# RWKV-7 scan on one TensorE: one 128x192 product for a chunk's masked products and transposes

## The chip, the cores and the metric

The kernel runs on one core of one Trainium2 chip. The time is the device time of one execution in microseconds (us), as the median of three runs. A profile of one further execution shows what each engine did: TensorE (PE, with its weight loads as PEld), VectorE (DVE), ScalarE (ACT), GpSimd (POOL), and SyncE (SP), whose queue issues most DMAs.

## The reference, cut to what matters

The program is a two-layer encoder for 256 + 1024 tokens of width 1024 in float32: an RWKV-7 layer, a neighbourhood attention layer, each followed by an MLP with 4096 hidden channels. The change concerns the recurrence of the first layer. For each of 16 heads and both directions of time it computes

```python
def step(S, inp):
    r_t, w_t, k_t, v_t, a_t, b_t = inp
    sa = jnp.einsum('bhvk,bhk->bhv', S, a_t)
    S = S * w_t[:, :, None, :] + sa[..., None] * b_t[:, :, None, :] + v_t[..., None] * k_t[:, :, None, :]
    return S, jnp.einsum('bhvk,bhk->bhv', S, r_t)
```

with a 64x64 state S per head. The output y of both directions is added, normalised per head (group norm with gain `lnx_g` and offset `lnx_b`), and a bonus times v is added to it.

## The kernel before

**Stages.** `l0_proj` makes r, k, v and the decay factors of all tokens and stores four scaled copies a, r (in `ar_d`) and b, k (in `bk_d`) to DRAM, per channel tile of 128 (two heads), direction and token. `scan` runs the recurrence. `channel_layer` and `attention` do the rest, and the change leaves them alone.

**The scan.** Time is cut into chunks of L = 64 tokens. Within a chunk the recurrence is products of 64x64 matrices; only the state S goes from chunk to chunk. Two heads lie in partitions 0 to 63 and 64 to 127, so a step's products are 64x64 quarters of the TensorE array; `HALVES` lists the two halves `es` and the opposite ones `eo`. There are ten jobs (`scan_job`) of 16 chunks, each job in 16 steps (`scan_step`); one step treats one chunk forward and one backward. The chunks of a job come in groups of four, g = 0 to 3, per direction d.

**What each (d, g) needs before its steps.** `prod` (L806) makes the masked a-b products; POOL and DVE then invert them (`mtr`, `rank1`, `qst`, some 36 steps ahead), and `merge1` and `merge2` (L899, L910) complete the inverse Q. `kload` (L928) loads r and k; a and b are still in SBUF from `load` (L801). `kprod` (L934) makes the products b-r into the bank `bps` and k-a, k-r into the bank `kps`; DVE multiplies them with the causal masks into `zr` (L951) and `zk` (L948). `ktr` (L953) transposes b and k through products with the identity into `lbps` and `lkps`; ACT copies them out as `lb` and `lk` (L964).

**One step** (L1005 to L1068): `s0` multiplies masked products and transposed k with v, ahead of time; `s1` multiplies a and r with the state S and adds S itself through the identity into the next state's bank `sn`; `s1c` copies the sum on ACT (`up`, L1034); `s2` multiplies Q with `up`; `s2c` copies it on ACT (`u`, L1045); `s3` multiplies transposed b and masked b-r with `u`; `s3c` scales `sn` into the new S on ACT (L1060, one instruction per direction); `s4` stores or adds the output y (L1066, L1068). S, `up`, `u`, S is a serial loop between PE and ACT.

**After eight chunks** `scan_post` normalises y on DVE and ACT, turns y and the bonus with `tr` (L1132, 16 products of 64x64 each) into `zps` and `vps`, applies gain and offset on ACT (`trc`, L1141), adds on DVE (`p5`, L1145) and stores with two DMAs (L1147).

**What sets the order.** In this stage every piece is put on a list with a time in steps, `at(t, f)`; the list is sorted by time and written out under `manual_schedule`, so each of PE, DVE, ACT and POOL runs its instructions in that written order. SP issues its DMAs in the order of the list too. Every engine stops at an instruction whose input or buffer isn't ready, and what is behind it waits.

**PSUM.** Eight banks: three in rotation under the tag `aps` (pool `pa`, for `aps`, `yps`, `qps`, `bps`, `kps`, `lbps`, `lkps`, `zps`, `vps`), one for A, two each for Y and for `sn` with U.

Of the kernel before, what the change touches and what calls it, by code (L numbers as in the profile page):

```python
# [29 lines left out]
V_QG, V_KG, V_LG, V_LB = 136, 137, 138, 146  # L30
NVEC = 154
# [18 lines left out]
class Trunk:  # L50
# [50 lines left out]
    def l0_proj(self):  # L101
# [253 lines left out]
        self.pa = self.pt = self.sctx.enter_context(tc.tile_pool(name="pa", bufs=3, space=PSUM, reuse_waits="tile"))  # L355
# [50 lines left out]
        def rmm(m, s):  # L406
            c0, c1 = SEGS[s]
            ps = ev[m, s] = self.pa.tile([P, 512], F32, name="rps", tag="aps")
# [37 lines left out]
        def vmm(i):  # L446
            q, tb = i // 10, i % 10
            vw = [tuple(z[:, k % 2 * 256:k % 2 * 256 + 256] for z in wq["v", q, k // 2]) for k in range(KT)]
            ev[i] = self.v_block(act, vw, v_d, (vp, "vt", 256, 2), (self.pa, "aps"), q, tb, later=True)
# [49 lines left out]
    def v_block(self, act, vw, dst, tp, pp, q, tb, scale=1.0, later=False):  # L499

        nc = self.nc
        ps = pp[0].tile([P, 512], F32, name="vps", tag=pp[1])
# [210 lines left out]
    def scan_begin(self):  # L713
# [10 lines left out]
        self.r_aa, self.r_bb, self.r_za = ([[er.tile([P, 4, 64], F32, name=f"{name}{i}") for i in range(9)], 0] for name in ("aa", "bb", "za"))  # L724
# [19 lines left out]
    def scan(self):  # L744
# [10 lines left out]
        for r, name in ((self.r_aa, "aa"), (self.r_bb, "bb"), (self.r_za, "za")):  # L755
            grow(r, name, [P, 4, 64], 12)
# [5 lines left out]
        self.b_a = self.pw.tile([P, 512], F32, name="ba")  # L762
        self.b_y, self.b_s = ([self.pw.tile([P, 512], F32, name=f"{nm}{i}") for i in range(2)] for nm in ("by", "bs"))
# [13 lines left out]
    def scan_job(self, j):  # L777
# [19 lines left out]
        for n, (d, g) in enumerate(order):  # L797
# [3 lines left out]
            def load(d=d, g=g, m=m, c0=c0):  # L801
                J["aa", d, g], J["bb", d, g] = self.nxt(self.r_aa), self.nxt(self.r_bb)
                nc.sync.dma_start(J["aa", d, g], c4(self.ar_d[m, d, 0, :, tok(c0)]))
                nc.sync.dma_start(J["bb", d, g], c4(self.bk_d[m, d, 0, :, tok(c0)]))

            def prod(h, d=d, g=g):  # L806
                if h == 0:
                    J["pa"] = w4(self.pa.tile([P, 512], F32, name="aps", tag="aps"))
                if h < 2:
                    for c in (2 * h, 2 * h + 1):  # L810
                        for es, eo in HALVES:
                            mm(J["pa"][es, c], J["bb", d, g][es, c], J["aa", d, g][es, c], start=True, stop=True)  # L812
# [83 lines left out]
        for n, (d, g) in enumerate(order):  # L896
# [27 lines left out]
            for dt, f in ((0.7, lambda f=merge1: f(0)), (0.72, lambda f=merge1: f(2)), (1.2, merge1c), (1.7, lambda f=merge2: f(0)), (1.72, lambda f=merge2: f(2)), (2.2, merge2c)):  # L924
                at(t + dt, f)


            def kload(d=d, g=g, m=m, c0=c0):  # L928
                J["rr", d, g] = self.rp.tile([P, 4, 64], F32, name="rr", tag="rr", bufs=8)
                nc.sync.dma_start(J["rr", d, g], c4(self.ar_d[m, d, 1, :, tok(c0)]))  # L930
                J["kk", d, g] = self.rp.tile([P, 4, 64], F32, name="kk", tag="kk", bufs=3)
                nc.sync.dma_start(J["kk", d, g], c4(self.bk_d[m, d, 1, :, tok(c0)]))

            def kprod(h, d=d, g=g):  # L934
                aa, rr, bb, kk = (J[x, d, g] for x in ("aa", "rr", "bb", "kk"))
                if h == 0:
                    J["pb"] = w4(self.pa.tile([P, 512], F32, name="bps", tag="aps"))
                    J["pk"] = self.pa.tile([P, 4, P], F32, name="kps", tag="aps")
                if h < 2:
                    for c in (2 * h, 2 * h + 1):  # L940
                        for es, eo in HALVES:
                            mm(J["pb"][es, c], bb[es, c], rr[es, c], start=True, stop=True)
                            mm(J["pk"][eo, c, 0:64], kk[es, c], aa[es, c], start=True, stop=True)
                        for es, eo in HALVES:
                            mm(J["pk"][eo, c, 64:128], kk[es, c], rr[es, c], start=True, stop=True)
                elif h == 2:
                    zk = J["zk", d, g] = self.rp.tile([P, 4, P], F32, name="zk", tag="zk", bufs=5)
                    nc.vector.tensor_tensor(out=zk, in0=J["pk"], in1=b4(self.mask[d], P), op=ALU.mult)  # L948
                else:
                    zr = J["zr", d, g] = self.rp.tile([P, 4, 64], F32, name="zr", tag="zr", bufs=5)  # L950
                    nc.vector.tensor_tensor(out=zr, in0=J["pb"], in1=b4(self.mask[d][:, 64:128], 64), op=ALU.mult)  # L951

            def ktr(h, d=d, g=g):  # L953
                if h == 0:
                    J["pl"] = [w4(self.pa.tile([P, 512], F32, name=nm, tag="aps")) for nm in ("lbps", "lkps")]
                if h < 2:
                    for c in (2 * h, 2 * h + 1):
                        for es, eo in HALVES:
                            mm(J["pl"][0][es, c], J["bb", d, g][es, c], self.ident[es, es], start=True, stop=True)
                            mm(J["pl"][1][eo, c], J["kk", d, g][es, c], self.ident[es, es], start=True, stop=True)  # L960
                else:
                    nm = ("lb", "lk")[h - 2]
                    lt = J[nm, d, g] = self.rp.tile([P, 4, 64], F32, name=nm, tag=nm, bufs=5)
                    nc.scalar.copy(lt, J["pl"][h - 2])  # L964
            t = 2 * n - 6
            at(t - 3.0, kload)
            for h, (dt, dl) in enumerate(((0.06, 1.4), (0.65, 1.41), (0.8, 1.65), (0.81, 1.85))):
                at(t + dt, lambda h=h, f=kprod: f(h))
                at(t + dl, lambda h=h, f=ktr: f(h))
# [21 lines left out]
    def scan_step(self, at, J, st, grp, k, i, new, end):  # L991
# [10 lines left out]
        def banks():  # L1002
            return pair(self.b_a), pair(self.b_y[k % 2]), pair(self.b_s[k % 2]), pair(self.b_s[k % 2][:, P:2 * P])

        def s0():  # L1005
            A, Y, sn, U = banks()
            for d, g, c, cc, m, ch in dirs:
                zk, v, yd = J["zk", d, g], J["v"], 1 - d if second else d
                for es, eo in HALVES:
                    mm(A[es, d], zk[eo, c, 0:64], v[eo, cc], d == 0, new)  # L1010
                    mm(Y[eo, yd], zk[eo, c, 64:128], v[eo, cc], d == 0, False)
                if not end:
                    for es, eo in HALVES:
                        mm(sn[es, d], J["lk", d, g][eo, c], v[eo, cc], d == 0, False)

        def s1():
# [4 lines left out]
            for d, g, c, cc, m, ch in dirs:  # L1021
                yd = 1 - d if second else d
                for es, eo in HALVES:
                    mm(A[es, d], J["aa", d, g][es, c], S[es, d], False, True)
                    mm(Y[eo, yd], J["rr", d, g][es, c], S[es, d], False, False)
            if not end:
                for d in range(2):
                    for es, eo in HALVES:
                        mm(sn[es, d], self.ident[es, es], S[es, d], False, False)
# [6 lines left out]
        def s2():  # L1036
            A, Y, sn, U = banks()
            for d, g, c, cc, m, ch in dirs:
                for es, eo in HALVES:
                    mm(U[es, d], J["Q"][es, cc, d], R["up"][es, d], end and d == 0, True)  # L1040
# [6 lines left out]
        def s3():  # L1047
            A, Y, sn, U = banks()
            for d, g, c, cc, m, ch in dirs:
                yd = 1 - d if second else d  # L1050
                for es, eo in HALVES:
                    if not end:
                        mm(sn[es, d], J["lb", d, g][es, c], R["u"][es, d], False, True)
                    mm(Y[eo, yd], J["zr", d, g][es, c], R["u"][es, d], False, True)
# [17 lines left out]
        at(i + 0.3, s2)  # L1072
        at(i + 0.38, s2c)
# [5 lines left out]
    def scan_post(self, at, J, grp, left):  # L1079

        nc = self.nc
        for half in range(2):
# [49 lines left out]
            def tr(src, nm, st=st):  # L1132
                ps = st[nm] = self.pa.tile([P, 8, 64], F32, name=nm, tag="aps")
                for b in range(8):
                    for es, eo in HALVES:
                        nc.tensor.matmul(ps[es, b], src()[eo, b // 4, b % 4], self.ident[eo, eo], start=True, stop=True)

            def trc(st=st, runs=runs):
                zt = st["zt"] = self.yp.tile([P, 8, 64], F32, name="zt", tag="zt", bufs=1)
                for x, (m, c0) in enumerate(runs):  # L1140
                    nc.scalar.activation(zt[:, 4 * x:4 * x + 4], st["zps"][:, 4 * x:4 * x + 4], AF.Identity, scale=self.v(V_LG, m), bias=self.v(V_LB, m))  # L1141

            def p5(st=st, runs=runs):
                zt = st["zt"]
                nc.vector.tensor_tensor(out=zt, in0=st["vps"], in1=zt, op=ALU.add)  # L1145
                for x, (m, c0) in enumerate(runs):
                    nc.sync.dma_start(self.scr["z_d"][m, :, c0 * L:(c0 + 4) * L], zt[:, 4 * x:4 * x + 4].rearrange("p c t -> p (c t)"))  # L1147
# [3 lines left out]
            else:  # L1151
                when = (0.2, 0.6, 0.95, 1.15, 1.45, 1.6, 1.75, 1.95, 2.3, 2.9, 2.95, 3.15, 3.45)
# [717 lines left out]
def host_layout(inputs):  # L1870
# [26 lines left out]
        col(i["rw_lnx_g"]), col(i["rw_lnx_b"])], 1)  # L1897
# [36 lines left out]
```

## Time and profile before

| what | value |
|---|---|
| median of three runs | 4189.79 us (4187.66 to 4193.83) |
| the profiled execution's own time | 4190.85 us |
| its span in the profile | 4189.1 us |
| granted TensorE clock, mean | 0.959 |
| busy: DVE, ACT, POOL (share of the span) | 2466.7 us (59%), 1537.4 us (37%), 1139.3 us (27%) |
| first and last product of a scan step (L993) | 756.7 us, 1451.1 us |
| steps in the scan | 160 |

Read it so: the span is what the profile covers, and 1.75 us of the execution's time lie around it. Busy shares are averages over stages with different limits, so the prediction goes to the stage between 757 and 1451 us and reads the engines and the waits there. A PE record is half of a float32 product: each such product stands in the trace as two weight loads and two multiplications.

### The profile page before, as it was taken

Reading aid. Unit: us, or ns where it says so; the run is one execution under the profiler, and the core shown is the slowest. Engines: PE = TensorE matmul, PEld = TensorE weight load, DVE = VectorE, ACT = ScalarE, POOL = GpSimd, SP = SyncE. Lnnn points to the kernel's source line nnn. Section 1 sums busy time; section 2 is a strip of 40 time slices with the busy share of each in tenths; the row PEclk is TensorE's granted clock in tenths of the full one; section 3 lists DMA queues with packets and bytes.
Section 4 is the critical chain, followed back from the end, with each engine's and each line's share of the span. In section 5 each row is a group of like instructions: output and inputs, shape, how many; then the busy total and the mean of one; then the engine's idle time right before and its main releaser. Section 6 shows DMA issues by size and latency. Waiting matters only on the chain.

```text
span 4189.1 us, 97599 instructions
## 1 busy us (share of the span) xinstructions
PE 3808.8 (91%) x40500; PEld 3201.6 (76%) x40500; DVE 2466.7 (59%) x4870; ACT 1537.4 (37%) x3671; POOL 1139.3 (27%) x998
## 2 busy tenths in 40 slices
PE   7897879777777799999999999989989999999999
PEld 4664669666777687888888879867767788888888
DVE  7888973556556357555555562366665755555555
ACT  6776651344444442111111133455564311111111
POOL 5440001011010134222222241244344422222222
PEclk8997889899999999999999999999998999999999
DMA  3326554654453251111011115332334111111011
GB/s 110 88 95 205 197 192 142 150 128 124 124 126 98 71 170 46 41 41 39 33 41 41 41 43 167 99 77 69 79 94 147 61 36 36 41 41 41 36 36 61
DMA packets 408092, 367.44 MB, mean 88 GB/s; under 512 B 203456, under 2 KB 332704, under 8 KB 407648
## 3 DMA queue, kind: packets, MB, share of 16 engines
q1 hardware_dynamic: 359136, 293.95, 24.1%
q10 hardware_dynamic: 46704, 61.35, 4.2%
q8 instruction: 318, 5.21, 0.5%
q0 software_dynamic: 1808, 5.90, 0.4%
q14 instruction: 126, 1.03, 0.1%
HBM read 251.07 MB, written 121.24 MB: 89 GB/s over the span
## 4 chain that ended last, share of the span: by engine, by line
PE 70%; DVE 15%; issue 5%; ACT 4%; DMA 4%; POOL 1%; SPq 1%; ACTq 0%; DVEq 0%; POOLq 0%
PE ps L96 17%; PE ps L97 17%; PE ps L98 17%; PE bs L993 2%; DVE q L860 1%; PE ba L993 1%; PE vps L506 1%; DVE tmp L858 1%; PE vps L507 1%; PE vps L508 1%; PE by L993 1%; PE op L1849 1%; PE aps L812 1%; PE pt L1791 1%; DVE mu L187 1%
## 5 line engine op out<-in xcount | busy, mean ns | idle before, releaser
L1406 DVE TENSOR_TENSOR x<-ps,x 128x256 f32<-128x256 f32 x1488 | 813.2, 594 | 629.8 <-PE ps L98 629.7
L96 PE MATMUL ps<-ah,whi 128*128 128x512 f32 (+1 forms) x2304 | 841.8, 365 | 4.8 <-ACT whi L90 4.2
L98 PE MATMUL ps<-ah,wlo 128*128 128x512 f32 (+1 forms) x2304 | 823.6, 357 | 2.2 <-POOL wlo L91 2.2
L97 PE MATMUL ps<-al,whi 128*128 128x512 f32 (+1 forms) x2304 | 823.0, 357 | 0.0
L91 POOL TENSOR_TENSOR wlo<-raw,whi 128x1024 fp32r<-128x1024 f32 (+1 forms) x178 | 389.9, 2190 | 858.0 <-ACT whi L90 829.9
L96 PE MATMUL ps<-hh,whi 128*128 128x512 f32 (+1 forms) x1536 | 547.4, 356 | 12.4 <-DVE x L1406 12.2
L98 PE MATMUL ps<-hh,wlo 128*128 128x512 f32 (+1 forms) x1536 | 546.1, 356 | 0.0
L97 PE MATMUL ps<-hl,whi 128*128 128x512 f32 (+1 forms) x1536 | 546.1, 356 | 0.0
L96 PEld LDWEIGHTS ps<-ah,whi 128*128 128x128 f32 x2304 | 436.7, 190 | 80.9 <-issue 13.1
L98 PEld LDWEIGHTS ps<-ah,wlo 128*128 128x128 f32 x2304 | 436.5, 189 | 68.1 <-POOL wlo L91 2.8
L97 PEld LDWEIGHTS ps<-al,whi 128*128 128x128 f32 x2304 | 438.0, 190 | 61.2 <-issue 1.1
L90 ACT CAST whi<-raw 128x1024 fp32r<-128x1024 f32 (+1 forms) x206 | 200.8, 975 | 699.2 <-PE ps L97 631.1
L96 PEld LDWEIGHTS ps<-hh,whi 128*128 128x128 f32 x1536 | 291.3, 190 | 56.5 <-DVE x L1406 15.5
L97 PEld LDWEIGHTS ps<-hl,whi 128*128 128x128 f32 x1536 | 291.6, 190 | 41.1
L98 PEld LDWEIGHTS ps<-hh,wlo 128*128 128x128 f32 x1536 | 291.4, 190 | 40.9
L1385 POOL TENSOR_TENSOR rl<-rl 128x512 f32<-128x512 f32 (+1 forms) x192 | 173.9, 906 | 499.9 <-PE ps L98 459.9
L1384 ACT ACTIVATE rl<-ps 128x512 f32<-128x512 f32 (+1 forms) x192 | 100.8, 525 | 544.1 <-PE ps L98 544.1
L1387 ACT CAST hh<-rl 128x512 fp32r<-128x512 f32 (+1 forms) x192 | 105.5, 550 | 321.4 <-POOL rl L1385 321.3
L1388 DVE TENSOR_TENSOR hl<-rl,hh 128x512 fp32r<-128x512 f32 (+1 forms) x192 | 119.3, 622 | 150.8 <-ACT hh L1387 150.5
L1784 POOL TENSOR_TENSOR s<-s,mx 128x384 f32<-128x384 f32 (+1 forms) x154 | 116.8, 769 | 207.6 <-DVE mx L1783 136.3
L1068 DVE TENSOR_TENSOR y<-by,y 128x128 f32<-128x128 f32 x80 | 24.7, 309 | 164.7 <-PE by L993 164.6
L1782 ACT ACTIVATE s<-s,mx 128x384 f32<-128x384 f32 (+1 forms) x154 | 87.1, 567 | 79.0 <-DVE mx L1781 77.6
(317 smaller groups left out, 8341.3 us busy)
## 6 DMA issues: line engine op xcount, KB each, us to landing
raw<-in_w_down_dram SPq DMA_DIRECT2D x64, 512.0 KB, 3.2
raw<-in_w_up_dram SPq DMA_DIRECT2D x64, 512.0 KB, 3.3
ar_d<-ar ACTq DMA_DIRECT2D x32, 512.0 KB, 2.8
bk_d<-bk ACTq DMA_DIRECT2D x32, 512.0 KB
bs<-tab SPq DMA_DIRECT2D x128, 96.0 KB, 3.5
v_d<-vt ACTq DMA_DIRECT2D x80, 128.0 KB, 3.5
aa<-ar_d SPq DMA_DIRECT2D x80, 128.0 KB, 3.0
bb<-bk_d SPq DMA_DIRECT2D x80, 128.0 KB, 2.8
```

What stands on the lines that cost most here:

```text
L90: nc.scalar.copy(hi[:, cs], raw)
L91: lo_eng.tensor_tensor(out=lo[:, cs], in0=raw, in1=hi[:, cs].bitcast(F32), op=ALU.subtract)
L96: mm(ps, sh, mh, start=first, stop=False)
L97: mm(ps, sh, ml, start=False, stop=False)
L98: mm(ps, sl, mh, start=False, stop=last)
L993: mm = lambda out, a, b, start, stop: nc.tensor.matmul(out, a, b, start=start, stop=stop, skip_group_check=True)
L1384: nc.scalar.activation(r[:, :n], ps[:, :n], AF.Relu)
L1385: nc.gpsimd.tensor_tensor(out=r[:, :n], in0=r[:, :n], in1=r[:, :n], op=ALU.mult)
L1387: nc.scalar.copy(hh[:, :n], r[:, :n])
L1388: nc.vector.tensor_tensor(out=hl[:, :n], in0=r[:, :n], in1=hh[:, :n].bitcast(F32), op=ALU.subtract)
L1406: nc.vector.tensor_tensor(out=xv, in0=ps[:, :n], in1=xv, op=ALU.add)
L1784: nc.gpsimd.tensor_tensor(out=s[:, :nk], in0=s[:, :nk], in1=mx[:, 2:3].to_broadcast([P, nk]), op=ALU.mult)
```

## The change

- **Products.** b and k of a chunk are laid side by side in one tile (`bk`, 128 columns: the weights), and a, r and an identity of 64 columns in another (`ar`, 192 columns: what moves). One product per chunk and half gives b-a, b-r, k-a, k-r and both transposes at once. It replaces `kprod` and `ktr` and has its own pair of banks (`pk2`, one buffer), one product pair of chunks per step. One DVE instruction masks the products of a pair of chunks (`kmask`), one ACT instruction copies the transposes (`kcopy`).
- **Loads.** `kload` loads all four of a, r, b, k: six DMAs where there were two, since b and k change sides between the halves. `load` keeps its two, into four buffers (`ea`, `eb`) of their own.
- **Turns.** `tr` turns two chunks at once: four products of 128x128 with a swapped identity for 16 of 64x64. Gain and offset then need four ACT instructions for two, and the store eight DMAs for two. `zt` has two buffers for one, and the turn of the bonus and what follows it come about a step later.
- **Banks.** `aps` two instead of three in the scan (while `l0_proj` still runs, a third bank `pax` is taken in turn by r and v); `sn` lies beside A, U beside Y; two banks each, four in all.
- **Order.** The merges come about a step earlier; S through the identity moves from `s1` to behind `s2`; within `s0` the state's part goes first.

```diff
-        self.pa = self.pt = self.sctx.enter_context(tc.tile_pool(name="pa", bufs=3, space=PSUM, reuse_waits="tile"))
+        self.pa = self.pt = self.sctx.enter_context(tc.tile_pool(name="pa", bufs=2, space=PSUM, reuse_waits="tile"))
+        pax = vctx.enter_context(tc.tile_pool(name="pax", bufs=1, space=PSUM, reuse_waits="tile"))
...
+        self.r_ar, self.r_bk = [[], 0], [[], 0]
+        grow(self.r_ar, "ar", [P, 12, 64], 8)
+        grow(self.r_bk, "bk", [P, 4, 2, 64], 5)
+        for t in self.r_ar[0]:
+            for es, eo in HALVES:
+                nc.gpsimd.tensor_copy(t[es, 8:12], self.ident[es, es].unsqueeze(1).to_broadcast([64, 4, 64]))
...
-            for dt, f in ((0.7, lambda f=merge1: f(0)), (0.72, lambda f=merge1: f(2)), (1.2, merge1c), (1.7, lambda f=merge2: f(0)), (1.72, lambda f=merge2: f(2)), (2.2, merge2c)):
+            for dt, f in ((-0.28, lambda f=merge1: f(0)), (-0.26, lambda f=merge1: f(2)), (0.15, merge1c), (0.42, lambda f=merge2: f(0)), (0.44, lambda f=merge2: f(2)), (0.9, merge2c)):
...
+                ar, bk = J["ar", d, g], J["bk", d, g] = self.nxt(self.r_ar), self.nxt(self.r_bk)
+                for x in range(2):
+                    for e, (es, eo) in enumerate(HALVES):
+                        nc.sync.dma_start(bk[es, :, x ^ e], c4(self.bk_d[m, d, x, es, tok(c0)]))
+                    nc.sync.dma_start(ar[:, 4 * x:4 * x + 4], c4(self.ar_d[m, d, x, :, tok(c0)]))
+            at(2 * n - 9.0, kload)
...
+            def kprod(c, g=g, d=d, pr=pr):
+                if c == 0:
+                    J["kp"] = self.pk2.tile([P, 2, 512], F32, name="kps", tag="kps")
+                ar, bk = J["ar", d, g].rearrange("p (x c) t -> p x c t", c=4), J["bk", d, g].rearrange("p c x t -> p c (x t)")
+                for e, (es, eo) in enumerate(HALVES):
+                    mm(J["kp"][:, e, 192 * c:192 * c + 192], bk[es, 2 * pr + c], ar[es, :, 2 * pr + c], start=True, stop=True)
...
+                nc.vector.tensor_tensor(out=z, in0=src[:, :, :, :P], in1=self.mask[d].unsqueeze(1).unsqueeze(1).to_broadcast([P, 2, 2, P]), op=ALU.mult)
...
+                nc.scalar.copy(z, src[:, :, :, P:])
+            t = q - 4.0
+            for dt, f in ((0.7, lambda f=kprod: f(0)), (0.72, lambda f=kprod: f(1)), (0.95, kmask), (1.15, kcopy)):
+                at(t + dt, f)
...
+        at(i + 0.32, s2b)
...
-                for b in range(8):
-                    for es, eo in HALVES:
-                        nc.tensor.matmul(ps[es, b], src()[eo, b // 4, b % 4], self.ident[eo, eo], start=True, stop=True)
+                swap = self.ident.rearrange("p (e t) -> p e t", e=2)[:, ::-1]
+                for b in range(4):
+                    nc.tensor.matmul(ps[:, b], src()[:, b // 2, b % 2 * 2:b % 2 * 2 + 2], swap, start=True, stop=True)
...
+                    for par in range(2):
+                        for e in range(2):
+                            nc.sync.dma_start(dst[e, :, c0 + par:c0 + 4:2], zt[64 * par:64 * par + 64, 2 * x:2 * x + 2, e])
...
-                when = (0.2, 0.6, 0.95, 1.15, 1.45, 1.6, 1.75, 1.95, 2.3, 2.9, 2.95, 3.15, 3.45)
+                when = (0.2, 0.6, 0.95, 1.15, 1.45, 1.6, 1.75, 1.95, 2.3, 3.15, 4.15, 3.3, 4.4)
```

Read as written order of the changed kernel: `kprod` stands between `s3` of one step and `s1` of the next; in every second step `merge1` is interleaved with it (two products of 128x192, four of 64x64, two, four). `kcopy` stands on ACT between `up` and `u`, and it waits for DVE's `kmask`.

More of the change, by code (lines that the diff above doesn't have):

```diff
@@ L407, in rmm @@
             c0, c1 = SEGS[s]
-            ps = ev[m, s] = self.pa.tile([P, 512], F32, name="rps", tag="aps")
+            ps = ev[m, s] = bank("rps")
             for k in range(KT):
@@ L448, in vmm @@
             vw = [tuple(z[:, k % 2 * 256:k % 2 * 256 + 256] for z in wq["v", q, k // 2]) for k in range(KT)]
-            ev[i] = self.v_block(act, vw, v_d, (vp, "vt", 256, 2), (self.pa, "aps"), q, tb, later=True)
+            ev[i] = self.v_block(act, vw, v_d, (vp, "vt", 256, 2), bank, q, tb, later=True)
         for i in range(40):
@@ L934, in kprod @@
[L934 to L940, printed above, removed]
-                        for es, eo in HALVES:
[L942 to L964, printed above, removed]
@@ L1002, in banks @@
         def banks():
-            return pair(self.b_a), pair(self.b_y[k % 2]), pair(self.b_s[k % 2]), pair(self.b_s[k % 2][:, P:2 * P])
+            x, y = self.b_x[k % 2], self.b_y[k % 2]
+            return pair(x), pair(y), pair(x[:, P:2 * P]), pair(y[:, P:2 * P])
+        zz = lambda d, g, c, e: J["zz", d, g, c // 2][:, c % 2, e]
+        ll = lambda d, g, c, e: J["ll", d, g, c // 2][:, c % 2, e]
         def s0():
             A, Y, sn, U = banks()
+            v = J["v"]
             for d, g, c, cc, m, ch in dirs:
[L1008 to L1014, printed above, removed]
+                for e, (es, eo) in enumerate(HALVES):
+                    if not end:
+                        mm(sn[es, d], ll(d, g, c, e)[eo], v[eo, cc], d == 0, False)
+            for d, g, c, cc, m, ch in dirs:
+                yd = 1 - d if second else d
+                for e, (es, eo) in enumerate(HALVES):
+                    mm(Y[eo, yd], zz(d, g, c, e)[eo, 64:128], v[eo, cc], d == 0, False)
+                    mm(A[es, d], zz(d, g, c, e)[eo, 0:64], v[eo, cc], end and d == 0, new)
         def s1():
@@ L1023, in s1 @@
                 for es, eo in HALVES:
[L1024 to L1029, printed above, removed]
+                    mm(Y[eo, yd], J["ar", d, g][es, 4 + c], S[es, d], False, False)
+                    mm(A[es, d], J["ar", d, g][es, c], S[es, d], False, True)
         def s1c():
@@ L1039, in s2, with s2b @@
                 for es, eo in HALVES:
-                    mm(U[es, d], J["Q"][es, cc, d], R["up"][es, d], end and d == 0, True)
+                    mm(U[es, d], J["Q"][es, cc, d], R["up"][es, d], False, True)
+        def s2b():
+            A, Y, sn, U = banks()
+            S = R["S"]
+            if S is None or end:
+                return
+            for d in range(2):
+                for es, eo in HALVES:
+                    mm(sn[es, d], self.ident[es, es], S[es, d], False, False)
         def s2c():
```

64 lines of the change are left out of this document (34 added, 30 removed).

## The prediction

> **What bounds the kernel now.** I read the page first, then the table of stages, then the chain of waits inside the scan. The profiled execution took 4190.85 us, 1.06 us over the median of the runs shown; my sum is made against it.
>
> ```profile
> span 4189.1 us, 97599 instructions
> PE 3808.8 (91%) x40500; PEld 3201.6 (76%) x40500; DVE 2466.7 (59%) x4870; ACT 1537.4 (37%) x3671; POOL 1139.3 (27%) x998
> PE   7897879777777799999999999989989999999999
> ```
>
> TensorE is full behind slice 15 and at 0.7 in the scan (slices 7 to 13), so PE's total says nothing of this stage. By stage (span, then busy time and count of PE, PEld, DVE, ACT, POOL, then granted clock and DMA share):
>
> ```profile
> 757.00:1440.00 683.00, 529.38 (x21392) 481.93 (x21387) 384.25 (x1025) 308.11 (x1166) 66.75 (x98) 0.96 0.46 117
> 1099.60:1139.20 39.60, 30.82 (x1188) 28.56 (x1188) 32.41 (x92) 17.87 (x70) 2.11 (x2) 0.91 0.40 110
> 1139.20:1172.90 33.70, 25.43 (x1085) 23.07 (x1076) 10.04 (x22) 13.70 (x52) 5.33 (x10) 1.00 0.57 134
> ```
>
> The second and third rows are one job: eight steps in which DVE also inverts the next job's matrices and normalises the last one's output ("heavy", 4.95 us a step), and eight without that ("light", 4.21 us). In the heavy half DVE is busy 82% (32.41 of 39.60 us). In the light half neither PE nor DVE is full; its chain of waits says what is late, and the instruction queue's row (packets, MB, share; whole scan) says why:
>
> ```profile
> by line: issue 25.2%; PE bs L993 17.2%; PE ba L993 10.4%; PE by L993 8.9%; PE lbps L959 6.8%; PE aps L812 6.7%; PE kps L945 4.0%; PE bps L942 3.8%; PE qps L916 3.4%; PE kps L943 3.4%; PE yps L904 2.8%; PE lkps L960 2.3%; DVE y L1105 1.8%; A
> q8 instruction: 168, 2.75, 1.7%
> ```
>
> "issue" is PE waiting for nothing in the data. 21392 + 21387 = 42779 PE instructions by 168 packets are 255 each, and 683 / 168 = 4.07 us is one packet. In the light half PE runs 2161 / 33.70 = 64 instructions a us, which is again 255 in 4.0 us. So I read the light half as bound by the delivery of PE's instructions, about 256 in 4 us, and the heavy half mostly by DVE. The Trainium skill ("Runtime: NRT & Kernel Launch", Instruction fetch mechanics) also gives 16 KiB blocks of 256 instructions, but says that crossing into one is mostly hidden; by that rule fewer instructions would gain nothing. The 25.2% speaks against it here.
>
> One step, as the timeline shows it:
>
> ```profile
> 1001.20 0.27 PE L993 MATMUL ba<-S,aa 64*64 64x64 f32 x1
> 1001.85 0.27 ACT L1034 COPY up<-ba 128x128 f32<-128x128 f32 x1
> 1003.13 0.27 PE L945 MATMUL kps<-rr,kk 64*64 64x64 f32 x1 [0.63 <-issue]
> 1003.14 0.27 PE L993 MATMUL bs<-up,qq 64*64 64x64 f32 x2
> 1003.69 0.27 ACT L1045 COPY u<-bs 128x128 f32<-128x128 f32 x1 [1.30 <-PE bs L993]
> 1004.01 0.27 PE L993 MATMUL bs<-u,lb 64*64 64x64 f32 x1
> 1004.52 0.52 ACT L1060 ACTIVATE S<-bs,dall 128x64 f32<-128x64 f32 x2 [0.56 <-PE by L993]
> 1004.93 0.28 PE L993 MATMUL by<-S,rr 64*64 64x64 f32 x2
> ```
>
> The bare loop is 0.65 to `up`, 0.27, 0.06 to `s2`, 0.55 to `u`, 0.27, 0.05 to `s3`, 0.51 to S, 0.41 to the next `s1`: 2.77 us. Everything above that is PE's other work in the holes of the loop, or a stall.
>
> **The change part by part.** *Instructions.* These go (records; a weight load stands beside each):
>
> ```profile
> L942 PE MATMUL bps<-rr,bb x1280: 213/219/367, 738.6 to 1429.4; 64*64 64x64 f32 x183
> L943 PE MATMUL kps<-aa,kk x1280: 212/219/366, 739.1 to 1429.4; 64*64 64x64 f32 x183
> L945 PE MATMUL kps<-rr,kk x1280: 212/219/313, 739.3 to 1429.6; 64*64 64x64 f32 x183
> L959 PE MATMUL lbps<-cst,bb x1280: 213/219/366, 744.4 to 1432.8; 64*64 64x64 f32 x183
> L960 PE MATMUL lkps<-cst,kk x1280: 212/219/365, 744.2 to 1432.8; 64*64 64x64 f32 x183
> L1136 PE MATMUL zps<-cst,y x640: 212/219/366, 821.2 to 1463.6; 64*64 64x64 f32 x160
> L1136 PE MATMUL vps<-cst,bv x640: 217/219/312, 824.1 to 1465.3; 64*64 64x64 f32 x160
> ```
>
> 6400 records of products become 640 products of two records, 1280; 1280 records of turns become 320. That is 6080 fewer, 12160 instructions with their loads, of about 42779: a step falls from 267 to some 210, delivered in 210 / 64 = 3.3 us. Delivery stops being the limit; what is late next is PE in its written order.
>
> *PE time of the product.* The cadence in one quarter of the array, in a half array with 128 columns, and the switch between shapes:
>
> ```profile
> 1000.05 0.22 PE L960 MATMUL lkps<-cst,kk 64*64 64x64 f32 x1
> 1000.11 0.22 PE L960 MATMUL lkps<-cst,kk 64*64 64x64 f32 x1
> ...
> 408.31 0.70 PE L610 MATMUL l<-tw,wa 64*128 64x256 f32 x4
> 408.84 0.60 PE L610 MATMUL l<-ta,wa 64*128 64x256 f32 x4
> ...
> 2742.68 0.28 PE L97 MATMUL ps<-al,whi 128*128 128x256 f32 x1
> 2742.79 0.28 PE L98 MATMUL ps<-ah,wlo 128*128 128x256 f32 x1
> 2743.00 0.88 PE L1849 MATMUL op<-s,vs 128*64 128x128 f32 x12
> 2743.81 0.39 PE L96 MATMUL ps<-ah,whi 128*128 128x256 f32 x1
> 2744.04 0.28 PE L97 MATMUL ps<-al,whi 128*128 128x256 f32 x1
> 2744.15 0.28 PE L98 MATMUL ps<-ah,wlo 128*128 128x256 f32 x1
> ```
>
> A 64x64 record takes 0.058 us of its quarter, and four quarters run at once. Of the 64-row records two run side by side, a pair in about 0.21 us for 256 columns (0.60 less 0.38 of one record's length, for two pairs); 12 records of 128 columns take six pairs at 0.10. So 192 columns take some 0.157 us, and the four products of a step 4 x 0.157 = 0.63 us. A change of shape costs besides: 0.21 for 0.12 going in, 0.81 for six pairs (0.65) inside, 0.23 for 0.11 coming out, together 0.09 + 0.16 + 0.11, about 0.33 us there and back. The Trainium skill ("TensorEngine Tiling (Array Packing)", Key Properties) says that a change of tiling mode drains TensorE; the rows agree, and the rule speaks against this change, which mixes shapes in a stage that had one. Before: kps took eight of the two off-diagonal quarters' turns, lbps and lkps four beside each other, (16 + 8) x 0.058 = 1.40 us in two steps. Now: 0.63 + 0.33 in one step, 0.63 + 2 x 0.33 in the other, where the merge splits it: 2.25. PE works longer with fewer instructions.
>
> *The light step.* With 0.23 for a block that fills its quarters twice (s1, s2, s2b, s3), 0.47 for s0, for aps and for qps, 0.23 + 0.23 for yps: in one step s2 starts at 0.98 (aps lies before it, hidden), s2 + s2b + s0 end at 1.86, qps at 2.33, s3 at 2.56, the product at 3.52; S is ready at 2.33 + 0.92, hidden. In the other s3 ends at 2.09, and product and yps (1.29 + 0.47) at 3.85. The mean is 3.69; for cold restarts and late banks I add 0.15 of the present stalls: 3.84, eight steps 30.7 for 33.7: **-3.0 us a job**.
>
> *The heavy half.* DVE's masks and the wait that the turns make there:
>
> ```profile
> L948 DVE TENSOR_TENSOR zk<-kps,cst 128x512 f32<-128x512 f32 x77 | 53.1, 689 | 55.2 <-PE kps L945 51.8
> L951 DVE TENSOR_TENSOR zr<-bps,cst 128x256 f32<-128x256 f32 x77 | 31.8, 414 | 0.0
> L1145 DVE TENSOR_TENSOR zt<-vps,zt 128x512 f32<-128x512 f32 x18 | 12.4, 688 | 29.8 <-DMA bb<-bk_d 10.8 <-PE vps L1136 10.4 <-ACT zt L1141 6.6
> ```
>
> One mask of 512 columns a step for 689 + 414 in two: +0.14 us a step, +1.1 in eight. The second `zt` and the later vps take off up to 29.8 / 18 = 1.7 us twice a job; I count 2.4. Against it the turns in 128x128 (8 x 0.10 + 0.33 = 1.2 us for 16 x 0.058 = 0.94) now stand before s2, and four `trc` in place of two before u: some 1 us net. Together -0.3 us; bounds -2.5 (DVE's 7.2 us idle shrink) and +2 (nothing freed). `kmask` is a new wait: `kcopy` and behind it on ACT u wait for it. In a light step the mask ends 0.95 after s1, the copy at 1.4, u is due at 1.53: hidden by 0.1; if DVE is late, u is as late.
>
> *Loads.* SP's issues:
>
> ```profile
> L930 SPq DMA_DIRECT2D rr<-ar_d x80: 319/431/1935, 735.7 to 1387.8; - x80
> L932 SPq DMA_DIRECT2D kk<-bk_d x80: 319/383/1824, 736.2 to 1407.8; - x80
> ```
>
> A job has some 64 issues and gets 32 (loads) and 12 (stores) more, 108 x 0.41 = 44 us of 67: hidden while loads lead by 2.5 steps or more. Start: the first products wait for six issues instead of two, and 16 POOL copies of the identity; last stores: six issues more. I take +6 us (bounds 0, 12). The banks of r and v before the scan rotate as before: 0.
>
> **Sum**: nine full jobs (the first two start afresh every four steps, the last has no successor's inversion) x (-3.0 - 0.3) = -30, +6: **-24 us, 4166.9 us** by the profiled execution.
>
> **The rivals.** (1) *Delivery was all.* If switches hide in the waits for S, u and up, light steps reach 3.3 us (-7.3 a job) and the heavy half -2: 9 x -9.3 + 6 gives 4113 us. For it: 25.2% issue. Against: the product stands where PE has no hole so long, 0.96 us for 0.69. (2) *One bound for another.* If a switch costs 0.1 us more than these rows, six in two steps make 4.14 a light step; the gain is 0.6 a job, and with a heavy half at zero 4191 us: no change. For it: DVE's load rises, TensorE's too. (3) *SP becomes the bound*: slower. In steps 7 to 9 the 12 loads of Q, 12 of keys and two of a and b come together, 26 issues in 7.7 us. At 0.41 us they lag 3 us, within a's and b's lead of 2.5 steps less some 3 us of flight, about 6.5 us. From 0.55 us an issue on the lag passes the lead, aps waits in PE's order, and every step with it: at 0.8 us 20.8 - 7.7 - 6.5 = 6.6 us a job, 9 x 6.6 = 59 on top of the forecast, 4226 us. For it: maxima of 1.9 us; against: medians of 0.41.
>
> **How the numbers follow.** Forecast 0.43 (its own range 4140 to 4182), rival 1 0.14, rival 2 0.18, rival 3 0.25. A measurement of this kernel tells about 0.2% (8 us) from no change. Faster: 0.43 + 0.14 = 0.57; within: 0.18; slower: 0.25. The range goes from 4108 (rival 1 and some heavy-half gain) to 4226 (rival 3), which leaves out about 0.07 below and 0.1 above.
>
> **What would show it.** Right: in the light half issue falls to a few per cent of the chain, about 210 PE instructions a step, light steps near 3.8 us, kps starting some 0.1 us late after s3 and s1 as late after it; heavy half within 2 us. Wrong: issue stays (delivery isn't by count); light steps at 3.3 (switches hidden) or over 4.1 (dearer, or u waits for kmask); aps or kps waiting for DMAs (rival 3).

## The result and the profile after

The changed kernel takes 4283.47 us (median of four runs, 4274.80 to 4289.81) for 4190.41 us before on the same chip: a ratio of 1.022, interval 1.020 to 1.024. It is slower by 93 us, where 24 us less was forecast; the range ended at 4226.

The page of the changed kernel, and its scan in the table of stages (span, then busy time and count of PE, PEld, DVE, ACT, POOL, then granted clock, DMA share, GB/s):

```profile
span 4288.0 us, 86148 instructions
PE 3915.4 (91%) x34420; PEld 3246.5 (76%) x34420; DVE 2488.2 (58%) x4870; ACT 1550.5 (36%) x3711; POOL 1140.7 (27%) x1014
...
PE 68%; DVE 13%; DMA 6%; ACT 5%; SPq 4%; issue 3%; POOL 2%; ACTq 0%; DVEq 0%; POOLq 0%
```
```profile
757.00:1536.00 779.00, 633.15 (x15792) 520.24 (x15794) 414.23 (x1049) 326.50 (x1219) 70.69 (x105) 0.87 0.55 129
...
1116.30:1133.50 17.20, 15.90 (x496) 13.14 (x496) 5.29 (x12) 8.66 (x33) 3.17 (x6) 1.00 0.51 123
1133.50:1144.10 10.60, 5.01 (x96) 4.35 (x96) 1.56 (x4) 1.42 (x5) 0.00 (x0) 0.68 0.64 143
```

PE has 6080 records fewer, as counted. The span grew by 98.9 us, and the scan's last step begins some 86 us later. Two stretches of one job stand below it: five light steps that take 17.2 us (3.44 each), and the one step behind them, which takes 10.6 us alone while PE is busy for 5.0. The clock of the scan fell from 0.95 to 0.87.

The steps of a job from the starts of `up` (means over the eight middle jobs, for step 15 over the first seven of them, us; from the 160 rows of that instruction in each trace; the prediction's light steps are 6 to 13, its heavy half 14, 15 and 0 to 5):

| steps | before | changed |
|---|---|---|
| 0, 1 | 4.20, 6.69 | 8.80, 6.93 |
| 2, 3 | 3.71, 6.40 | 4.37, 3.56 |
| 4, 5 | 3.81, 3.61 | 7.51, 5.41 |
| 6 to 10, sum | 20.3 | 17.3 |
| 11 | 4.22 | 8.07 |
| 12 to 15, sum | 18.2 | 18.7 |

Steps 6 to 10 gained 0.6 us each, steps 2 and 3 together 2.2. The loss stands in two places, the four steps that hold the new turns (0, 1, 4, 5: +10.3) and step 11 (+3.9). PE's waits in the scan, grouped (engine, line, tile waited with, what ended it: us, times, longest), before and after:

```profile
PE bs L993 <- ACT up L1034: 23.5, 31, 2.4
PE by L993 <- issue: 15.0, 20, 1.5
PE bs L993 <- issue: 13.0, 17, 1.9
```
```profile
PE aps L824 <- DMA eb<-bk_d: 47.5, 17, 6.1
PE by L994 <- ACT up L1036: 46.6, 74, 2.2
PE bx L994 <- ACT u L1056: 29.2, 28, 2.6
```

The waits for instruction delivery ("issue"), 76.2 us over all lines before, are 0.2 us. A load that comes late (`eb`) and u are there in their place, and `up` is waited for twice as long. Why the load is late stands on SP's own timeline of the job above (start, length, instruction, count):

```profile
1114.10 6.55 SPq L1163 DMA_DIRECT2D z_d<-zt  x8
...
1127.48 1.94 SPq L904 DMA_DIRECT2D qx<-qd  x2
1129.47 1.54 SPq L905 DMA_DIRECT2D qq<-qd  x3
...
1133.92 1.55 SPq L905 DMA_DIRECT2D qq<-qd  x3
1135.57 0.43 SPq L830 DMA_DIRECT2D dd<-za  x1
1136.05 0.50 SPq L815 DMA_DIRECT2D ea<-ar_d  x1
1136.60 0.44 SPq L816 DMA_DIRECT2D eb<-bk_d  x1
```
```profile
1138.99 1.12 PE L824 MATMUL aps<-ea,eb 64*64 64x64 f32 x16 [5.58 <-DMA eb<-bk_d]
```

`eb` is issued at 1136.60, behind eight stores of z and the loads of Q; PE has stood since 1133.4 and goes on at 1138.99. SP's issues themselves became long as well as many (count, then min/median/max in ns):

```profile
L944 SPq DMA_DIRECT2D bk<-bk_d x320: 573/586/1923, 732.2 to 1498.6; - x160
L945 SPq DMA_DIRECT2D ar<-ar_d x160: 326/601/1908, 733.5 to 1485.9; - x160
L1163 SPq DMA_DIRECT2D z_d<-zt x160: 574/597/1640, 846.7 to 1556.3; - x160
```

Summed over the rows, the 996 issues that start between 757 and 1520 us take 635 us, a mean of 0.64; before, 571 issues took 325 us in 683, a mean of 0.57. At a turn the timeline reads (PE and ACT of step 0 of that job):

```profile
1080.84 1.65 PE L957 MATMUL kps<-ar,bk 64*128 64x192 f32 x8
...
1082.42 2.07 PE L1148 MATMUL zps<-cst,y 128*128 128x128 f32 x8
...
1083.66 0.37 ACT L967 COPY ll<-kps 128x256 f32<-128x256 f32 x1 [2.81 <-DVE zz L962]
...
1084.53 1.50 ACT L1154 ACTIVATE zt<-zps,vec 128x128 f32<-128x128 f32 x4 [0.49 <-PE zps L1148]
...
1085.91 0.28 ACT L1056 COPY u<-by 128x128 f32<-128x128 f32 x1
...
1086.24 0.27 PE L994 MATMUL bx<-u,ll 64*64 64x64 f32 x1 [0.67 <-ACT u L1056]
```
```profile
1114.88 0.92 PE L957 MATMUL kps<-ar,bk 64*128 64x192 f32 x8
```
```profile
1080.60:1088.90 8.30, 7.63 (x112) 6.00 (x111) 6.47 (x19) 3.00 (x11) 0.00 (x0) 0.69 0.65 163
```

The turn stands 2.07 us in front of s2. On ACT, `ll` (`kcopy`) waits 2.81 us until DVE has masked the product (`kmask`), then four `zt` take 1.50 us, and `u` stands behind both. The same product takes 1.65 us here and 0.92 us in the row of a later step: the clock of this step is 0.69 (last fence, third number from the end).

### The profile page after: what moved, and what is told of

Same layout as the page of the kernel before. It is cut to its first block, busy times and chain, and to the rows that moved or that the text cites. A ratio compares the mean times of both kernels' runs of the same rounds, so it can differ in the third digit from the quotient of the medians.

```text
span 4288.0 us, 86148 instructions
## 1 busy us (share of the span) xinstructions
PE 3915.4 (91%) x34420; PEld 3246.5 (76%) x34420; DVE 2488.2 (58%) x4870; ACT 1550.5 (36%) x3711; POOL 1140.7 (27%) x1014
## 4 chain that ended last, share of the span: by engine, by line
PE 68%; DVE 13%; DMA 6%; ACT 5%; SPq 4%; issue 3%; POOL 2%; ACTq 0%; DVEq 0%; POOLq 0%
PE ps L96 17%; PE ps L97 17%; PE ps L98 17%; PE kps L957 2%; PE by L994 2%; PE bx L994 1%; PE vps L512 1%; PE vps L513 1%; PE vps L514 1%; PE pt L1807 1%; PE op L1865 1%; DMA eb<-bk_d 1%; DVE cs L629 1%; PE yps L916 1%; DVE mu L187 1%
## 5 line engine op out<-in xcount | busy, mean ns | idle before, releaser
L962 DVE TENSOR_TENSOR zz<-kps,cst 128x512 f32<-128x512 f32 x160 | 110.3, 689 | 153.0 <-PE kps L957 152.9
L957 PE MATMUL kps<-ar,bk 64*128 64x192 f32 x1280 | 193.5, 404 | 0.1
```

Of the source, the lines that this page charges most:

```text
L957: mm(J["kp"][:, e, 192 * c:192 * c + 192], bk[es, 2 * pr + c], ar[es, :, 2 * pr + c], start=True, stop=True)
L962: nc.vector.tensor_tensor(out=z, in0=src[:, :, :, :P], in1=self.mask[d].unsqueeze(1).unsqueeze(1).to_broadcast([P, 2, 2, P]), op=ALU.mult)
```

## The experiments

Ratios are to the kernel before, run beside each group on one chip (its median there 4204 to 4212 us); a point is 1% of that time. The step sums are from one trace of each run. Two suspects stood at the start: SP's lag together with the turns (theory 1), or the wide product itself, by its switches and the clock.

**early_loads**: a and b of the inversion three steps earlier.

```diff
-            at(t - (1.4 if j else 4.0), load, E)
+            at(t - (4.4 if j else 4.0), load, E)
```

> The changed kernel with one edit: a and b of the inversion (ea, eb) are loaded 4.4 steps ahead of their step for 1.4 (every job but the first). Nothing else moves; the number of DMAs is the same. Theory 1 (SP's queue is late: 17 waits of aps for eb, 47.5 us, most of them in step 11, where SP issues 26 loads behind eight stores): the waits of aps go to under 10 us, step 11 falls from 8.1 to some 3.5 us, and some of the half-clock windows behind those waits go too: 4283 - 45 to -60 = 4225 to 4240 us. Rival (SP is late for everything alike; an earlier place only shifts which load is late: bk, ar, qq or the mt loads come late instead): under 15 us gained, above 4268 us, with a new DMA wait of the same size in the chain.

Measured: 1.0217 (1.0199 to 1.0234), nothing gained. Step 11 fell to 2.83 us, as theory 1 said; step 15 rose from 5.25 to 12.35 us. PE's largest wait, and the wait of DVE for mt that stands behind it:

```profile
PE by L994 <- DVE y L1079: 79.5, 8, 13.5
```
```profile
DVE q L866 <- POOL mt L854: 95.0, 7, 16.4
```

The matrices for the inversion (mt) now came late (34.4 us of such waits in the changed kernel), and DVE, in its written order, kept y waiting behind them. The rival held: another load is late in its place. That became theory 2: SP's issues of a job fill the job.

**old_turns**: turns, `zt`, stores and their times as before; the product stays.

```diff
-                for b in range(4):
-                    nc.tensor.matmul(ps[:, b], src()[:, b // 2, b % 2 * 2:b % 2 * 2 + 2], swap, start=True, stop=True)
+                for b in range(8):
+                    for es, eo in HALVES:
+                        nc.tensor.matmul(ps[es, b], src()[eo, b // 4, b % 4], self.ident[eo, eo], start=True, stop=True)
```

> The changed kernel with the turns, the gain and offset, the stores and their times as before (16 products of 64x64 for a turn, two ACT instructions, two stores, one zt, gains laid out as before); products, loads, banks and merges stay changed. Theory 1 (in steps 0, 1, 4 and 5 the turns cost: eight 128x128 records stand before s2, four zt instructions of ACT stand before u, and the two turns of a post fall in two steps): steps 0 to 5 fall from 36.6 us in sum to 28 to 31, and SP has 12 issues a job fewer, so the wait for eb shrinks by some 2 us a job: 9 x -8 to -10, 4193 to 4211 us. Rival (the wide product is what costs: the clock and the switches): steps 0 to 5 fall by less than 2 us, 4265 us or more, granted clock in the scan still near 0.87.

Measured: 1.0028 (1.0016 to 1.0041), 1.9 points gained; steps 0 to 5 sum to 28.4 us. But the edit takes both the turns and twelve stores of a job away, and waits for loads stayed (eb 30.4 us; steps 13 and 15 at 8.2 and 7.2).

**turns_only**: the reverse edit, in the kernel before.

> The kernel before with the new turns alone (four products of 128x128, four ACT instructions, eight stores, two zt, the later times of the changed kernel, gains laid out for it); products, loads, banks and merges are those of before. Theory 1 (the turns cost by themselves): steps 0 to 5 rise from 28.4 us in sum by 4 to 8: 4190 + 35 to 70, 4225 to 4260 us. Rival (the turns are harmless, and only together with the wide product, fewer banks and a full SP queue do they cost): within 10 us of 4190.

Measured: 1.0039 (1.0024 to 1.0054), 16 us slower; steps 0 to 5 sum to 32.6 us for 28.4. Less than theory 1 expected, more than its rival. Beside the product and with SP's queue as it is, the same edit costs 1.9 points, some 80 us (the changed kernel less old_turns).

**idle_records**: 14 products of one column more in each step, so that PE's instruction count is as before.

```diff
+            for x in range(14):
+                es, eo = HALVES[x % 2]
+                mm(self.b_y[k % 2][eo, 256 + x:257 + x], self.ident[es, es], R["u"][es, 0, x:x + 1], False, True)
```

> The changed kernel with 14 more products of 64x64 by one column in each step, behind s3, into columns that nothing reads: 28 records and 28 loads more, so that a step has some 266 PE instructions again, as before the change, for about 0.3 us of PE time. Theory 1 (the light steps gained because fewer instructions are delivered, 256 in about 4 us): issue is again over 10% of the light half's chain, and steps 6 to 10 go from 3.46 us on average back to 4.0 or more: 4283 + 25 to 45 us. Rival (the light steps gained by the order of merges, banks or products): issue stays under 3% and the steps rise by no more than the 0.3 us that the records take, to 3.75 at most: 4283 + 0 to 20 us.

Measured: 4356.66 us, one run. Steps 6 to 10 rose to 4.28 us on average, but the waits for delivery sum to only 3.2 us in the scan. On PE's timeline the added records stand so:

```profile
1145.86 0.89 PE L994 MATMUL by<-u,cst 64*64 64x1 f32 x25
```

25 of them, of one column, take 0.89 us (0.70 without the 0.19 of the last one's length, 24 distances of 0.029), so 28 take some 0.81 where 0.3 had been reckoned. The steps became longer by about the records' own time (4.28 for 3.46), PE asked for no more than 266 / 4.28 = 62 instructions a us, and stood at 64 before. The test doesn't decide.

**pool_bk**: GpSimd issues the 32 loads of b and k of a job.

```diff
-                        nc.sync.dma_start(bk[es, :, x ^ e], c4(self.bk_d[m, d, x, es, tok(c0)]))
+                        nc.gpsimd.dma_start(bk[es, :, x ^ e], c4(self.bk_d[m, d, x, es, tok(c0)]))
```

> The changed kernel, but GpSimd issues the 32 loads of b and k (bk) of a job in place of SP; the same DMAs, at the same place of the list. SP has 76 issues a job in place of 108. Theory 2 (SP's queue as a whole is full: 635 us of issues in 779 us of scan, the rest its own waits; so moving one load ahead only made another late): the waits of aps for eb (47.5 us) and of DVE for POOL's copy of mt (34.4 us) both fall under 10 us, steps 11 and 15 come under 4.5 us, ratio to before 1.006 to 1.012 in place of 1.022. Rival (the transfers are late, by their small packets, whoever issues them; or GpSimd's issues are slower still and its copies of mt are late): load waits of 40 us or more stay under other names, ratio 1.018 or more.

Measured: 0.9988 (0.9974 to 1.0002): 2.3 points, about 98 us, by who issues the same DMAs; theory 2 had expected less (1.006 to 1.012). The price of an issue on GpSimd, PE's wait for `eb`, and the scan:

```profile
L944 POOL DMA_DIRECT2D bk<-bk_d x320: 617/617/789, 735.3 to 1413.4; - x160
```
```profile
PE aps L824 <- DMA eb<-bk_d: 2.5, 1, 2.5
```
```profile
757.00:1457.00 700.00, 598.09 (x15776) 490.30 (x15776) 414.89 (x1049) 326.91 (x1220) 252.55 (x407) 0.92 0.60 143
```

An issue costs GpSimd about as much as SP (0.617 us for a median of 0.586), so it isn't the issuer's speed but the count on one queue. Nor are the transfers faster. From issue to landing `eb` takes, in the changed kernel and here:

```profile
DMA to landing us min/median/max: 2.3/2.9/5.2
```
```profile
DMA to landing us min/median/max: 2.3/5.0/7.6
```

It takes longer here, and PE hardly waits for it: what had been late was the issue. DVE's wait for mt fell from 34.4 to 14.5 us, not under the 10 expected. Steps 11 and 15 are 2.8 and 3.7 us, and the clock of the scan went from 0.87 to 0.92 with no change in PE's work. What stays are the steps of the turns (0, 1, 4, 5: 28.4 us in sum, 18.3 in the kernel before).

**before_pool**: the control, the kernel before with its loads of r and k (16 a job) issued by GpSimd.

```diff
-                nc.sync.dma_start(J["rr", d, g], c4(self.ar_d[m, d, 1, :, tok(c0)]))
+                nc.gpsimd.dma_start(J["rr", d, g], c4(self.ar_d[m, d, 1, :, tok(c0)]))
```

> The kernel before, with its 16 loads of r and k of a job issued by GpSimd in place of SP: the control for pool_bk. Theory 2 (SP was full only in the changed kernel; before it was busy 325 of 683 us): within 0.3% of before, ratio 0.997 to 1.003. Rival (loads off SP help any version of this scan, and pool_bk shows nothing of the change): ratio under 0.99.

Measured: 1.0020 (1.0011 to 1.0030). Before the change SP had room; taking loads off it brings nothing, and costs 0.2%.

**pool_z**: GpSimd issues the 16 stores of z instead; b and k are with SP again.

```diff
-                            nc.sync.dma_start(dst[e, :, c0 + par:c0 + 4:2], zt[64 * par:64 * par + 64, 2 * x:2 * x + 2, e])
+                            nc.gpsimd.dma_start(dst[e, :, c0 + par:c0 + 4:2], zt[64 * par:64 * par + 64, 2 * x:2 * x + 2, e])
```

> The changed kernel, but GpSimd issues the 16 stores of z of a job in place of SP: 16 x 0.68 = 10.9 us less for SP a job, half of what pool_bk took off. It parts what old_turns gained (1.9 points) into the queue's share and the turns' own. Theory 2: SP has then some 60 us of issues for a job of 75: 9 x 6 to 11 = 55 to 98 us gained, ratio 1.000 to 1.010. Rival (old_turns gained by the turns' time on PE and ACT, the stores are hidden): under 25 us gained, ratio 1.016 or more.

Measured: 1.0068 (1.0053 to 1.0084), 1.5 points, some 64 us; `eb` is waited for 19.7 us. So 10.9 us of issues less gain 7 us a job, 21 less (pool_bk) gain 11. Moving the stores alone gains 1.5 of the 1.9 points of old_turns, so the queue can account for most of these; with the queue relieved the turns still cost 1.2 points (pool_bk less product_pool, below).

**zt_behind**: `trc` in two parts, one `zt` between u and S, three behind S, none ahead of u.

```diff
-                when = (0.2, 0.6, 0.95, 1.15, 1.45, 1.6, 1.75, 1.95, 2.3, 3.15, 4.15, 3.3, 4.4)
+                when = (0.2, 0.6, 0.95, 1.15, 1.45, 1.6, 1.75, 1.95, 2.3, 3.15, 4.15, 3.55, 3.9, 4.4)
```

> The changed kernel with the four ACT instructions of gain and offset (zt) no longer ahead of u: one stands between u and S, three behind S. SP's work is unchanged. Theory 2 (SP's full queue sets the time of a job, steps 0 and 4 only take the place of waits): steps 0 and 4 fall by 1 to 2 us each, and the time comes back in the waits for loads (eb, mt): ratio 1.018 to 1.022, under 15 us gained. Rival (u behind zt is a cost of its own in the serial loop): 2 x 1.2 to 2 us a job, 9 jobs: 20 to 36 us gained, ratio 1.013 to 1.017.

Measured: 1.0145 (1.0125 to 1.0165), 0.75 points, some 31 us. Theory 2 had said under 15, its rival 20 to 36: a full queue doesn't hide everything on the serial loop. Part did go the way it said: steps 0 and 4 fell by 4.6 us a job in sum, the wait for `eb` rose from 47.5 to 69.4 us.

**pool_zt**: both edits.

> The changed kernel with both edits: b and k issued by GpSimd, zt behind u and S. Theory 2: with SP no longer full, the steps 0 and 4 of zt_behind count now: 15 to 30 us less than pool_bk, ratio 1.000 to 1.006; what stays is the turns' PE time in front of s2 (1.2 us, 2.0 at half clock, four a job). Rival (zt is hidden): within 8 us of pool_bk.

Measured: 0.9886 (0.9869 to 0.9902), 1.0 point below pool_bk, some 43 us: more than expected, and a version 48 us faster than before.

**product_pool**: old turns, and b and k by GpSimd: the product with room in every queue.

> The changed kernel with the old turns (as in old_turns, which gave a ratio of 1.003) and GpSimd issuing the loads of b and k: the wide product without turns and without a full SP queue. Theory 2: no waits for eb, mt or ar over 10 us in sum, steps 13 and 15 under 5 us (8.2 and 7.2 in old_turns), light steps 3.2 to 3.8: ratio 0.988 to 0.996, faster than before. Rival (the product itself loses what it gains, by its switches and half-clock windows): ratio 1.000 to 1.005.

Measured: 4153.25 us, 0.9869 (0.9853 to 0.9886), 55 us faster than before and the fastest of all. Steps 0 to 5 sum to 29.0 us (28.4 before), 6 to 10 to 17.9, 11 to 15 to 19.7 (22.4). Its scan, and SP's largest group of waits:

```profile
757.00:1411.00 654.00, 576.53 (x16642) 476.84 (x16641) 414.45 (x1048) 319.84 (x1184) 254.87 (x406) 0.94 0.65 153
```
```profile
SPq L945 <- PE bx L994: 82.6, 17, 13.3
```

SP waits up to 13.3 us for PE: it runs ahead again. In the changed kernel its largest group of that kind is this, and no wait of SP there is over 4.6 us:

```profile
SPq L944 <- PE by L994: 15.4, 34, 1.2
```

All of SP's waits in the scan sum to 137 us there, which with 635 us of issues fills its 779 us; they sum to 322 us here and to 367 in the kernel before, where a load of k waited so:

```profile
SPq L932 <- PE by L993: 22.2, 17, 6.7
```

**late_turns**: pool_zt with both turns behind s2 and `zt` in two pairs (times of the two turns, the two pairs and `p5`).

```diff
-                when = (0.2, 0.6, 0.95, 1.15, 1.45, 1.6, 1.75, 1.95, 2.3, 3.15, 4.15, 3.55, 3.9, 4.4)
+                when = (0.2, 0.6, 0.95, 1.15, 1.45, 1.6, 1.75, 1.95, 2.3, 3.44, 4.45, 3.9, 4.42, 4.7)
```

> The changed kernel with b and k issued by GpSimd, and with both turns moved behind s2 (into the time in which PE waits for u) and zt in two pairs, one behind S, one behind u of the next step; an attempt at the fastest version. Theory 2: the 1.2 to 2.0 us of a turn no longer stand before s2, so steps 0, 1, 4 and 5 fall by some 0.7 us each against pool_zt: 9 x 2.8 = 25 us, ratio 0.980 to 0.985. Rival (DVE sets the heavy steps, the turns' place is indifferent): ratio 0.986 to 0.991, as pool_zt.

Measured: 0.9921 (0.9905 to 0.9938), above both expectations and 0.35 points above pool_zt, which ran on another chip. Steps 0, 1, 4 and 5 sum to 24.2 us for 23.2. In step 0 `u` starts 3.18 us behind `up` for 3.29 in pool_zt, and in both it stands, in most of the eight jobs, right behind `ll`, which waits for DVE's mask. So a turn moved behind s2 frees nothing there; the next section has the numbers of this wait.

## Why the prediction was wrong

Two terms of the sum failed: the loads, counted as hidden, cost some 98 us, and the heavy half, counted at -0.3 us a job, lost some 50 us by the turns. The product itself gained more than forecast.

The parts, from the ratios: the product with room in the queues -1.31 points (product_pool), the turns as the change has them +1.19 (pool_bk less product_pool), SP's full queue +2.3 (after less pool_bk): +2.2 in sum (that they add up to the whole is by the way they are taken). In us about -55, +50, +98.

1. *Delivery (held in the trace, not tested alone).* With 12160 instructions fewer the waits for delivery went from 76.2 us (97 waits, 256 PE instructions or a multiple apart to within one) to 0.2. The Trainium skill ("Runtime: NRT & Kernel Launch", Instruction fetch mechanics) has such crossings mostly hidden; the trace disagrees by these 76.2 us, but the one experiment on it decided nothing.
2. *The product's price (right).* Forecast 0.96 us with a switch there and back, 1.76 us together with `yps` where the merge splits it; a row above shows 0.92 us, and below it is 1.81 us from the first product to the last part of `yps`, which stands between products of s1. (The three parts of the switch, 0.09 + 0.16 + 0.11, add up to 0.36 and not to 0.33; it changes little.)

```profile
1108.24 0.60 PE L957 MATMUL kps<-ar,bk 64*128 64x192 f32 x4
1108.77 0.45 PE L916 MATMUL yps<-qx,za 64*64 64x64 f32 x8
1109.15 0.60 PE L957 MATMUL kps<-ar,bk 64*128 64x192 f32 x4
1109.67 0.37 PE L916 MATMUL yps<-qx,za 64*64 64x64 f32 x2
...
1110.05 0.32 PE L916 MATMUL yps<-qx,za 64*64 64x64 f32 x2
```

3. *The light step (right sign, too small).* Forecast 3.84; steps 6 to 10 take 3.46 in the changed kernel, nearer to the 3.3 of rival 1. Over all of the prediction's light steps, 6 to 13, the mean is 3.61 in product_pool for 4.09 before, a gain of 3.9 us a job where 3.0 was forecast; in the changed kernel it is 4.35, for the late load in step 11. The 0.15 for restarts didn't come.
4. *The heavy half: the step that failed in size, with a wait that was put at nothing.* "Together -0.3 us" was counted, with bounds of -2.5 and +2. With SP relieved (pool_bk) steps 0 to 5 still sum to 36.1 us for 28.4: +7.7, where the product alone adds 0.6. The sum took "four `trc` in place of two before u" and the turns ahead of s2 as some 1 us net. But the two of the kernel before stood ahead of `up`, at the end of steps 15 and 3; the four now stand ahead of `u`. They take 1.50 us, at each of two turns a job; moving them behind u and S gained 31 us (zt_behind) and 43 us (pool_zt). The turn's own PE time was reckoned right for full clock, 1.2 us (1.16 in the row of `vps` at 1088.68); at half clock it is 2.07.

   The wait is that for `kmask`. The prediction called it "a new wait", "hidden by 0.1" in a light step, and gave it no price in the heavy half, though "if DVE is late, u is as late". In the changed kernel `ll` waits for it 2.75 us in step 0 and 1.84 in step 4 (means of the eight jobs), with `u` behind it; in pool_zt it is still 2.59 and 1.50, in product_pool nothing in these steps. ACT's waits for the mask in the whole scan, in the changed kernel, pool_zt and product_pool:

```profile
ACT ll L967 <- DVE zz L962: 83.6, 36, 5.7
```
```profile
ACT ll L967 <- DVE zz L962: 60.3, 32, 3.2
```
```profile
ACT ll L967 <- DVE zz L962: 12.6, 7, 5.2
```

No run moves `kmask` or `kcopy`, so what this wait costs by itself is not shown: with the old turns `up` comes later, and steps 2, 3 and 15 are longer instead (5.67, 6.13 and 4.59 us for 4.82, 3.68 and 3.51 in pool_zt).

5. *Loads: the step that failed in kind.* "108 x 0.41 = 44 us of 67: hidden while loads lead by 2.5 steps." The 0.41 was a median of issues of whole 128-partition tiles, and the mean of all issues in that same trace was 0.57. The new ones cost 0.59 to 0.60 in the median, and the mean of all was 0.64, by the tail up to 1.9 us that the prediction quoted against itself. 108 x 0.64 = 69 us, more than the 67 us of the job as forecast: the queue is full. Rival 3 named the mechanism and its point (0.55 us an issue), the wait (aps, here in step 11) and the sign; it had not counted the eight stores of z that stand ahead of those loads. It allowed 59 us on top of the forecast and the queue cost 98: of some 8 us a job that pool_bk takes off, 5.3 are in step 11 and 2.9 in steps 12 to 15, so not aps alone was late.
6. *What the sum left out: the clock.* But for 0.15 us a light step "for cold restarts and late banks" it took full clock everywhere. Here the granted clock is 1.00 (1116.3 to 1133.5 us) or 0.50 (1137.0 to 1143.5), and the mean of a stretch tells the mix. In the scan it is 0.87 for 0.95 before: (1 - 0.87) x 2 x 779 = 203 us of half clock. In pool_bk it is 0.92, in product_pool 0.94, in pool_zt 0.96, by the same reckoning 112, 78 and 53 us. pool_zt has the same product, so the product's shape alone doesn't bring the half clock. It is a price contained in the points above, and what brings it is shown in part only. The Trainium skill ("TensorE: Matmul & The Clock Gate", HAM oscillation) says that idle gaps of more than some 3.4 us halve the clock afterwards; the trace agrees where the wait of 5.58 us stands in a stretch at 0.68. But waits as long as that are found only among the 17 for `eb` (no other group of PE's waits has one over 2.7 us), and step 0 above is at 0.69 with no wait of PE over 1.5 us between 1070 and 1087.

What stays open: how much of the light steps' gain is delivery and how much the new order of merges and banks, which no run separates; what DVE's late mask costs by itself; what brings the half clock where PE's waits are short; and why the tail of SP's issues reaches 1.9 us.

## What to carry to other kernels

A change that saves instructions on one engine by finer data layouts pays in DMA issues: count the issues of a period on their queue, by the mean of their durations, tail included, against the length of that period as it will be after the gain. A queue that never waits long for its consumers (here 4.6 us at most, for 11.4 before) is likely full; then moving one load ahead can just make another late, as early_loads did, and a second issuer can be worth more, as in pool_bk. Work of ACT that is set between two links of a serial loop cost at least its length here (1.50 us twice a job, 27 us in nine jobs, for 31 and 43 gained), though ACT is busy 36% on the average. A wait that a forecast calls hidden by a tenth of a microsecond needs a price for the case that it isn't.

## What the runs showed that was not expected

- GpSimd issued 320 loads at 0.617 us each, with a maximum of 0.789; on SP the same loads had a median of 0.586 and a maximum of 1.923.
- Records of one column, in two quarters in turn, followed each other at 0.029 us, so at 0.058 in each quarter: as long as records of 64 columns take there.
- The granted clock moved from 0.87 to 0.92 by a change of the DMAs' issuer alone.
